# Sixteen small writes to the output ahead of the first load, on GpSimd's software queue

## The chip, the cores and the metric

The kernel runs on one core of a Trainium2 chip (trn2). Times are device microseconds (us) of that core; executions that agree within 1.5% of the fastest are fast. A packet below is one entry of the trace's record of the DMA engines, with its start, its length and its size. An "engine-us" is one microsecond of one of the sixteen DMA engines: 16 engine-us over all engines are 1 us of each.

## The reference, cut to what matters

```python
# attn_weights: (8, 12, 1024, 1024) float32;  v: (8, 12, 1024, 64) float32
def reference(attn_weights, v):
    return np.einsum('bhqs,bhsd->bhqd', attn_weights, v).astype(np.float32)
```

Almost all bytes are attention weights: 403 MB, read once. v and the output are 25 MB each.

## The kernel before

The 96 heads are handled four at a time, in 24 blocks. A block is a pair of attention loads (8.4 MB each in memory, cast to 16 bits on the way), one v load (1 MB) and one store (1 MB). GpSimd issues them all on its software queue, except the first v load and the last stores, which SyncE issues on its hardware queue. TensorE transposes the weights and multiplies.

```python
nc.vector.memset(ident, 0.0).then_inc(s_memset)
# ...
load_attn(0)                      # GpSimd, software queue
load_attn(1)
pool.wait_ge(s_memset, 2)
pool.affine_select(out=ident, ...)  # constants for TensorE
# ...
for n in range(NU - 2):
    pool.wait_ge(s_t[True], (n + 1) * PER_DVE)   # a buffer is free
    load_attn(n + 2)
    if n % 2 == 0:
        q = n // 2
        for s in s_sp:
            pool.wait_ge(s, 2 * q + 2)
        if q + 1 < NV:
            load_v(q + 1)
        if 0 < q <= HELD_FROM:
            store(q - 1)          # the first store: q = 1, at 79.5 us
# ...
nc.sync.dma_start(out=v32, in_=v_g[0]).then_inc(s_v0, 16)   # the first v, hardware queue
# ... at the end:
nc.sync.wait_ge(s_out, NU)
nc.sync.dma_start(out=outs[:, 0], in_=rows[:, 0]).then_inc(s_end, 16)
```

Of the kernel before, what the change touches and what calls it, by code (L numbers as in the profile page):

```python
# [10 lines left out]
def kernel(  # L11
# [18 lines left out]
    nc = tc.nc  # L30
# [16 lines left out]
    NV = NH // VH  # L47
# [12 lines left out]
    def slot(q):  # L60
        return q % 2 if q < 2 * BY_EIGHTS else q - 2 * BY_EIGHTS + 2

    attn_q = attn_weights.rearrange("b (hq four) (p r) s -> (b hq) (four p) (r s)", four=VH, p=VP)
    out_q = out.rearrange("b (hq four) (p r) d -> (b hq) (four p) (r d)", four=VH, p=VP)
    v_g = v.rearrange("b (hq four) (p r) d -> (b hq) (four p) (r d)", four=VH, p=VP)
# [11 lines left out]
    with tc.tile_critical(no_gpsimd_drain=True):  # L77
        sem = tc.alloc_semaphore
# [17 lines left out]
        s_second = {n: sem(f"s_second{n}") for n in range(HALVED, NU)}  # L96
        s_v0, s_v = sem("s_v0"), sem("s_v")
        s_osb = [sem(f"s_osb{i}") for i in range(NO)]
        s_end = sem("s_end")

        s_t = {True: sem("s_t_dve"), False: sem("s_t_act")}
        s_sp = [sem("s_sp_dve"), sem("s_sp_act")]
# [109 lines left out]
        def engine(dve):  # L212
# [11 lines left out]
            def back_copy(rows, j0, jn, ps, count):  # L224

                eng.wait_ge(s_back, count)
                return copy(  # L227
                    out=rows.rearrange("p (half j) d -> p j half d", half=2)[:, ds(j0, jn)],
                    in_=ps[:, ds(0, jn * P)].rearrange("p (j half d) -> p j half d", half=2, d=D),
                )  # L230

            def rows_of(n):
                return osb[slot(n // 2)][:, ds(n % 2 * G, G)]
# [51 lines left out]
            k = 1 - e  # L285
            back_copy(rows_of(NU - 1), 4 * k, 4, px[k], 2 * NU + k + 1).then_inc(s_fin[k])

        nc.vector.memset(ident, 0.0).then_inc(s_memset)
        nc.vector.memset(spread, 0.0).then_inc(s_memset)

# [23 lines left out]
        def store(q, by_sync=False):  # L314
# [12 lines left out]
            out=ident,  # L327
            in_=ident,
# [7 lines left out]
        for h in range(VH):  # L336
            pool.wait_ge(s_const, h + 1)
            pool.affine_select(  # L338
                out=spread[ds(h * VP, VP)],
                in_=spread[ds(h * VP, VP)],  # L340
# [39 lines left out]
            store(q, by_sync=True)  # L380
        rows = osb[slot(NV - 1)].rearrange("p (u half j) d -> p u half j d", u=2, half=2)
        outs = out_q[NV - 1].rearrange("p (u half j d) -> p u half j d", u=2, half=2, j=GH)
        nc.sync.wait_ge(s_out, NU)
        nc.sync.dma_start(out=outs[:, 0], in_=rows[:, 0]).then_inc(s_end, 16)
        for k in range(2):
# [36 lines left out]
```

## Time and profile before

| | before |
|---|---|
| time, median of the first 3 runs | 1055.67 us (1055.58 to 1055.79) |
| span of the profiled run | 1053.3 us |
| software queue's share of the sixteen engines | 99.4% |
| TensorE starts on the first load | 25.21 us |
| second pair of loads landed | 86.63 us |
| interval with the first store / with every later one | 45.06 / 43.56 us |

The lines behind these are in the prediction. TensorE's start tells when the first load landed. It is in the timeline (start, busy, engine, line, operation):

```profile
25.21 9.57 PE L124 MATMUL bank<-ident,abf 128*128 128x128 f32 x64 [25.21 <-DMA abf<-in_attn_weights_dram]
```

An interval is the time between the landings of two pairs of loads, each read from the chain in order of time as start plus length.

### The profile page before, as it was taken

To read this page: it belongs to the slowest core of one execution; us is meant where nothing else is said; L and a number is where in the kernel's file an instruction comes from. 1 tells how busy PE (TensorE), PEld (TensorE's weight loads), DVE (VectorE), ACT (ScalarE), POOL (GpSimd) and SP (SyncE) were. 2 spreads that over 40 slices of the span, in tenths; PEclk is the share of its full clock that TensorE was granted. 3 is DMA by queue.
4 is the path that set the end of the run, shared out by engine and by line. 5 is a ranking of instruction groups with operands and counts; after the bars stand their busy time and mean duration, and the time that the engine had idled before them with its cause. 6 is when DMAs were issued, how large, how long until landed. Compare 5 with 4: busy or idle time off the path is not lost.

```text
span 1053.3 us, 16277 instructions
## 1 busy us (share of the span) xinstructions
PE 754.8 (72%) x6920; PEld 709.4 (67%) x6920; DVE 387.9 (37%) x582; ACT 403.3 (38%) x489; POOL 52.4 (5%) x102
## 2 busy tenths in 40 slices
PE   0877686766867578775687766876678768777795
PEld 0776576766867568675686666866667668776785
DVE  1443343333443234432343333433335234433452
ACT  0443344433543334442353333433334334433452
POOL 1000000000000000000000000000000000000000
PEclk9989888888888888898888888888789898898898
DMA  9999999999999999999999999999999999999998
GB/s 219 220 217 208 234 236 218 238 209 247 233 218 238 207 243 239 217 238 209 244 236 215 234 219 237 238 219 234 227 228 234 215 218 218 218 218 215 210 217 322
DMA packets 14662, 239.67 MB, mean 228 GB/s; under 512 B 1600, under 2 KB 2112, under 8 KB 5184
## 3 DMA queue, kind: packets, MB, share of 16 engines
q0 software_dynamic: 13392, 234.36, 99.4%
q1 hardware_dynamic: 1264, 5.24, 1.3%
q8 instruction: 2, 0.03, 0.0%
q14 instruction: 4, 0.03, 0.0%
HBM read 427.82 MB, written 25.17 MB: 430 GB/s over the span
## 4 chain that ended last, share of the span: by engine, by line
DMA 76%; PE 23%; issue 1%; POOL 0%; DVE 0%; ACT 0%; SPq 0%; POOLq 0%
DMA abf<-in_attn_weights_dram 76%; PE bank L124 22%; PE bank L166 0%; PE bank L151 0%; POOL abf L304 0%; DVE osb L227 0%; ACT ot L256 0%; POOLq L417 0%; SPq L371 0%; SPq L77 0%
## 5 line engine op out<-in xcount | busy, mean ns | idle before, releaser
L124 PE MATMUL bank<-ident,abf 128*128 128x128 f32 x3072 | 470.8, 327 | 260.0 <-DMA abf<-in_attn_weights_dram 254.2
L124 PEld LDWEIGHTS bank<-ident,abf 128*128 128x128 f32 x3072 | 461.5, 215 | 272.8 <-DMA abf<-in_attn_weights_dram 266.7
L244 DVE COPY at<-bank 128x1024 bf16<-128x1024 bf16 x480 | 320.3, 689 | 495.1 <-PE bank L124 492.5
L244 ACT COPY at<-bank 128x1024 bf16<-128x1024 bf16 x288 | 289.2, 1012 | 428.1 <-PE bank L124 428.1
L166 PE MATMUL bank<-at,vbf 128*64 128x256 bf16 x3072 | 215.0, 278 | 0.0
L166 PEld LDWEIGHTS bank<-at,vbf 128*64 128x64 bf16 x3072 | 196.7, 108 | 13.4 <-DVE at L244 4.0
L256 ACT COPY ot<-bank 128x512 f32<-128x512 f32 x48 | 28.1, 586 | 181.1 <-PE bank L166 181.1
L256 DVE COPY ot<-bank 128x512 f32<-128x512 f32 x48 | 33.2, 692 | 151.4 <-PE bank L166 151.4
L151 PE MATMUL bank<-ident,ot 128*128 128x128 f32 x392 | 52.2, 276 | 33.0 <-DVE vbf L220 32.2
L151 PEld LDWEIGHTS bank<-ident,ot 128*128 128x128 f32 x392 | 43.4, 141 | 45.0 <-DVE vbf L220 44.0
L304 POOL DMA_DIRECT2D abf<-in_attn_weights_dram x50 | 26.6, 532 | 896.4 <-PE bank L124 895.3
L227 ACT COPY osb<-bank 128x512 f32<-128x512 f32 x97 | 52.2, 589 | 22.5 <-PE bank L151 22.5
L220 DVE CAST vbf<-bank 128x512 bf16<-128x512 f32 x48 | 30.9, 686 | 6.6 <-PE bank L139 6.6
L220 ACT CAST vbf<-bank 128x512 bf16<-128x512 f32 x48 | 25.8, 589 | 11.8 <-PE bank L139 11.8
L139 PE MATMUL bank<-vr,spread 32*128 32x512 bf16 x384 | 25.7, 377 | 0.0
L139 PEld LDWEIGHTS bank<-vr,spread 32*128 32x128 bf16 x384 | 9.9, 92 | 6.9
L310 POOL DMA_DIRECT2D vr<-in_v_dram x23 | 12.1, 528 | 19.2 <-PE bank L139 18.8
L317 POOL DMA_DIRECT2D out_dram<-osb x20 | 10.7, 537 | 37.3 <-ACT osb L227 37.3
L244 ACT ACT_TABLE_LOAD x8 | 10.3, 1283 | 1.2 <-SPq L77 1.1
L294 DVE CAST vr<-v 128x2048 bf16<-128x2048 f32 x1 | 1.4, 1406 | 3.3 <-DMA v<-in_v_dram 3.3
L338 POOL TENSOR_SCALAR_AFFINE_SELECT spread<-spread 32x512 bf16<-32x512 bf16 x4 | 2.5, 629 | 0.6
L227 DVE COPY osb<-bank 128x512 f32<-128x512 f32 x1 | 0.7, 692 | 3.1 <-PE bank L151 3.1
(8 smaller groups left out, 2.1 us busy)
## 6 DMA issues: line engine op xcount, KB each, us to landing
abf<-in_attn_weights_dram POOLq DMA_DIRECT2D x46, 4096.0 KB, 33.2
out_dram<-osb POOLq DMA_DIRECT2D x20, 1024.0 KB, 34.2
vr<-in_v_dram POOLq DMA_DIRECT2D x23, 512.0 KB, 34.3
abf<-in_attn_weights_dram POOLq DMA_DIRECT2D x4, 2048.0 KB, 26.0
out_dram<-osb SPq DMA_DIRECT2D x3, 1024.0 KB, 11.8
v<-in_v_dram SPq DMA_DIRECT2D x1, 1024.0 KB, 4.9
out_dram<-osb SPq DMA_DIRECT2D x1, 512.0 KB, 7.8
out_dram<-osb SPq DMA_DIRECT2D x2, 256.0 KB, 3.0
```

The source lines that it names most:

```text
L124: last = pe.matmul(out=pt[g % 4][:, k], lhsT=words[:, k], rhs=ident, is_transpose=True, start=(k == 0), stop=(k == KW - 1),)
L139: last = pe.matmul(out=ps, lhsT=spread[rows, b], rhs=vr[rows, b], start=(b == 0), stop=(b == VB - 1),)
L151: last = pe.matmul(out=ps[:, ds(j * P, P)], lhsT=ot[:, j0 + j], rhs=ident, is_transpose=True, start=(j == 0), stop=(j == jn - 1),)
L166: last = pe.matmul(out=outs, lhsT=vbf[:, 2 * kw + par, h], rhs=at[:, ds(half * GH, GH), kw, ds(h * VP, VP), par], start=(n == 0), stop=(n ...
L220: copy(out=vbf[:, :, h], in_=ps.rearrange("p (k d) -> p k d", k=SB)).then_inc(s_vbf[e])
L227: return copy(out=rows.rearrange("p (half j) d -> p j half d", half=2)[:, ds(j0, jn)], in_=ps[:, ds(0, jn * P)].rearrange("p (j half d) -> ...
L244: ins = copy(out=at[:, g].rearrange("c k j two -> c (k j two)"), in_=bank[g % 4].bitcast(bf16),)
L256: copy(out=ot.rearrange("c j (h p) -> c h j p", h=VH)[:, ds(2 * e, 2)], in_=po[e].rearrange("c (h j p) -> c h j p", h=2, j=GH),).then_inc( ...
L304: pool.dma_start(out=abf[n % 2][:, ds(g0, gn)].rearrange("p g s -> p (g s)"), in_=attn_q[n // 2][:, ds((n % 2 * G + g0) * S, gn * S)],).th ...
L310: pool.dma_start(out=vr.rearrange("p b x -> p (b x)"), in_=v_g[iv]).then_inc(s_v, 16)
L317: eng.dma_start(out=out_q[q], in_=osb[slot(q)].rearrange("p r d -> p (r d)"), **({} if by_sync else {"single_packet": True}),).then_inc(s_ ...
L338: pool.affine_select(out=spread[ds(h * VP, VP)], in_=spread[ds(h * VP, VP)], compare_op=mybir.AluOpType.not_equal, fill=1.0, base=0, patte ...
```

## The change

The sixteen pieces are 64 bytes each, one for each DMA engine, copied from v into places of `out` that the last stores overwrite. The intent: let every engine touch `out` once at the start, so that whatever a first write costs is paid early and not in the middle of the stream.

```diff
-        s_end = sem("s_end")
+        s_end, s_touch = sem("s_end"), sem("s_touch")
 # ... ahead of the first load on GpSimd:
+        nc.gpsimd.dma_start(
+            out=out_q[NV - 1].rearrange("(e p) x -> e p x", e=16)[:, 0, ds(0, 16)],
+            in_=v_g[0].rearrange("(e p) x -> e p x", e=16)[:, 0, ds(0, 16)],
+        ).then_inc(s_touch, 16)
 # ... before the last stores:
+        nc.sync.wait_ge(s_touch, 16)
         nc.sync.wait_ge(s_out, NU)
```

## The prediction

> **What bounds the kernel now.** I read the page first, for which resource is full.
>
> ```profile
> PE 754.8 (72%) x6920; PEld 709.4 (67%) x6920; DVE 387.9 (37%) x582; ACT 403.3 (38%) x489; POOL 52.4 (5%) x102
> q0 software_dynamic: 13392, 234.36, 99.4%
> HBM read 427.82 MB, written 25.17 MB: 430 GB/s over the span
> DMA 76%; PE 23%; issue 1%; POOL 0%; DVE 0%; ACT 0%; SPq 0%; POOLq 0%
> ```
>
> No compute engine is full, but packets of the software queue q0 take 99.4% of the span of the sixteen DMA engines, and the chain that ended last is 76% loads. The 23% of PE in that chain are transposes that free a buffer for the next load while another load already fills the engines. So time is bytes over rate: 427.82 + 25.17 = 453 MB at 430 GB/s give 1053 us. What matters is any stretch in which the engines do less than that.
>
> I then looked for such stretches. The chain in order of time (start, length, what) shows when pairs of loads land:
>
> ```profile
> 2.14 43.36 DMA abf<-in_attn_weights_dram
> ...
> 55.31 31.32 DMA abf<-in_attn_weights_dram
> ...
> 96.46 35.23 DMA abf<-in_attn_weights_dram
> ...
> 141.28 33.97 DMA abf<-in_attn_weights_dram
> ```
>
> Start plus length gives landings at 45.50, 86.63, 131.69 and 175.25, so intervals of 41.13, 45.06 and 43.56 us; the later ones with a store in them are also 43.56. The first interval has no store: 1 MB less, 2.4 us at 430 GB/s, accounts for 41.1. But the interval with the *first* store is 1.5 us longer than every later one. The stretches (bounds, length, each engine's busy time, PE clock, DMA share, GB/s delivered) compare its v load with the next pair's, each from its first packet:
>
> ```profile
> 104.20:105.20 1.00, 0.00 (x0) 0.00 (x0) 0.00 (x0) 0.00 (x0) 0.00 (x0) 0.50 0.88 139
> 105.20:106.20 1.00, 0.20 (x1) 0.20 (x2) 0.00 (x0) 0.00 (x0) 0.00 (x0) 0.50 1.12 123
> 106.20:107.20 1.00, 1.00 (x6) 1.00 (x6) 0.03 (x1) 0.00 (x0) 0.00 (x0) 0.50 0.78 115
> 148.60:149.60 1.00, 0.00 (x0) 0.00 (x0) 0.00 (x0) 0.00 (x0) 0.00 (x0) 0.50 0.56 111
> 149.60:150.60 1.00, 0.00 (x0) 0.00 (x0) 0.00 (x0) 0.00 (x0) 0.00 (x0) 0.50 0.93 188
> 150.60:151.60 1.00, 0.55 (x3) 0.55 (x4) 0.00 (x0) 0.00 (x0) 0.00 (x0) 0.50 1.08 266
> ```
>
> For 2.5 us the first delivers about half the rate of the second. The single packets say the same: a v packet takes 0.324 us everywhere, but here up to 0.96, an excess of 16 engine-us, or 1.0 us on each of 16 engines. No other stretch of the kernel has that much. The first store's packets follow at 107.5 us and themselves are normal (0.309 to 0.322 us).
>
> The timeline of the start (start, busy, queue) shows who issues first:
>
> ```profile
> 0.96 0.39 SPq L363 DMA_DIRECT2D v<-in_v_dram  x1
> 1.48 1.22 POOL L304 DMA_DIRECT2D abf<-in_attn_weights_dram  x2 [1.03 <-SPq L77]
> ```
>
> In the packet records the v load (queue q1) runs from 2.0 us; its first packets take 0.6 to 1.1 us, later ones 0.309. The first q0 packet starts at 5.04, on each engine 6 ns or so after that engine's last q1 packet (5.0 to 5.5). So **the first attention load waits for the v load, not for its own issue**.
>
> **What the Trainium skill says.** "DMA: Bandwidth & Descriptors", section "Where 436 GB/s comes from", puts the fabric ceiling at 435 GB/s; the trace's 430 agrees, and leaves an estimated 453 MB / 435 GB/s = 1041 us, so no change that leaves the bytes alone can gain much over 1%. The same page, "Specifications", says that software-issued transfers take about 1 us to the first byte and that pieces under 512 B are written by read-modify-write. The v load, hardware-issued, took 1.0 us from issue to first packet, longer than the 0.6 us given there; no run yet shows a small write. I found no page that names a cost for a first write to a tensor. "TensorE: Matmul & The Clock Gate", section "What's actually happening", says that the activity window is 3413 ns and runs free; the trace has a granted clock of 0.50 from 1034 us to about 1039.4 and 1.00 after.
>
> **The change part by part.** Nothing is removed. Added:
> 1. One issue on GpSimd ahead of the first load. An issue costs 0.49 to 0.73 us there (1.22 for two). The first load is issued near 2.0 instead of 1.48, its descriptors are ready at about 3.0 (estimate with the skill's 1 us), still before the v load ends at 5.04. On the path: **0 us**. The constants on GpSimd come 0.5 us later too, at 6.7 instead of 6.2; PE needs them at 25.2.
> 2. Sixteen packets of 64 B, one per engine by the 16-row pattern, with sixteen semaphore packets, ahead of the first load in the same queue. A 1 KB packet takes 0.046 us and a semaphore packet 0.022 in this trace, so **+0.07 us** if warm. If cold, like the first v packets (0.3 to 0.8 us over normal), **+0.3 to +0.8**.
> 3. A wait on SyncE near 1041 us, met since microsecond 6: 0. A branch on GpSimd: under 0.1 us, hidden as in 1.
> 4. If the 1.5 us at 104 is the engines' first write to out, the change pays that earlier: **-1.5**, less what it costs at the start. There the v load is running, so half-rate reads for 2.5 us could cost up to 1.2 again; or it overlaps the slow first v packets and costs little.
>
> A shift carries to the end one for one: the queue always holds another load (33 us to landing, against about 20 of transfer), and the tail follows the last landing at 1034.27.
>
> The sum: with the saving of 4, 1055.67 - 1.5 + 0.1 to 1.2, so 1054.3 to 1055.4. Without it, +0.1 to +0.8, so 1055.8 to 1056.5.
>
> **The rivals.** *First-write cost moved* (45%): for it speaks that the slow stretch comes just before the first store, whose descriptors had been waiting since 79.5 us, and never returns; against it, that it hits v reads and not the store's own packets. It gives about 1054.8. *Chance collision* (40%): around 104 us the engines, until then in step to within about 1 us, drift apart, and the v packets collide once with long reads. The touch then saves nothing except by chance: 1055.9. *The small write blocks the queue* (15%): read-modify-write and receipt hold each engine 1 to 2 us ahead of the first load, with no saving later: 1057. Against it, packets behind a store in this trace don't stall. On top lies the **clock phase in the tail**: the last transposes take 6.25 us because most run at clock 0.50; a shift against the free-running window could lengthen or shorten that by an estimated 1 us, though a gain stops at the DMA, which is 0.98 busy from 1034 to 1049.
>
> **Range and chances.** 0.45 x 1054.8 + 0.40 x 1055.9 + 0.15 x 1057 = 1055.6; I take 1055.4, as the first theory could pay more than I charge it. The range spans the full saving, 1054.1, to the blocking case, 1057.0. Two per cent is 21 us, more than the 12 us to the ceiling; a slowdown that large needs a lasting loss of rate from sixteen packets. Hence 0.98 for within 2%.
>
> **What would show it.** (1) The first load's landing (PE starts at 25.21 now) moves by 0.1 to 0.8 us, not by the issue's 0.5 plus more. (2) The landing interval with the first store drops from 45.06 to 43.56 if the first-write theory holds, and stays within 0.3 if not. (3) v at the start lands later than 4.9 us after issue if the cost moved there. (4) Later intervals stay at 43.56. (5) The tail from last landing to end keeps its 19 us. The prediction is wrong if the engines settle into another pattern with another steady interval: 0.5 us in each of 18 would be 9 us.

## More of the kernel before

"Slow engine-us" are the lengths of slow packets over their usual length, added up.

As the engines are always busy, intervals show where the run gains or loses. But a pair has landed only when the slowest of the sixteen engines is done. So an interval holds two things: what all engines lose, and how far the slowest falls behind the others.

## The result, and the profile after

| | before | after |
|---|---|---|
| time, median of 4 runs | 1055.73 us (1055.58 to 1056.07) | 1055.84 us (1055.79 to 1056.01) |
| ratio | | 1.0001, 95% interval 0.9984 to 1.0018 |
| span of the profiled run | 1053.3 us | 1053.6 us |
| TensorE starts on the first load | 25.21 us | 26.54 us |
| slow engine-us of loads in the first 10 us | 0.2 | 8.3 |
| interval with the first store | 45.06 us | 44.08 us |
| slow engine-us near the first store | 15.8 | 9.6 |

A ratio here is the mean time of one kernel's fast runs over that of the other's of the same rounds, so not quite the ratio of the medians in the table. The time is the same. But the two traces differ, in three places.

**The start.** The timeline after shows the added issue, the first load's issue 0.65 us later, and TensorE's start:

```profile
0.96 0.39 SPq L369 DMA_DIRECT2D v<-in_v_dram  x1
...
1.50 0.63 POOL L290 DMA_DIRECT2D out_dram<-in_v_dram  x1 [1.05 <-SPq L77]
...
2.13 1.10 POOL L310 DMA_DIRECT2D abf<-in_attn_weights_dram  x2
...
26.54 10.46 PE L124 MATMUL bank<-ident,abf 128*128 128x128 f32 x64 [26.54 <-DMA abf<-in_attn_weights_dram]
```

TensorE starts 1.33 us later. The stretches (bounds, length, busy time of PE, PEld, DVE, ACT, POOL, PE clock, DMA share, GB/s of packets that start there) show why. Each engine moves the first load in packets of usually 2.432 us; the second packets start here. Before:

```profile
7.40:8.10 0.70, 0.00 (x0) 0.00 (x0) 0.00 (x0) 0.00 (x0) 0.00 (x0) 1.00 3.48 749
8.10:9.40 1.30, 0.00 (x0) 0.00 (x0) 0.00 (x0) 0.00 (x0) 0.00 (x0) 1.00 0.00 0
```

After:

```profile
7.40:8.10 0.70, 0.00 (x0) 0.00 (x0) 0.00 (x0) 0.00 (x0) 0.22 (x1) 1.00 1.91 374
8.10:9.40 1.30, 0.00 (x0) 0.00 (x0) 0.00 (x0) 0.00 (x0) 0.00 (x0) 1.00 0.97 202
```

Before, all sixteen second packets start before 8.1 us: 749 GB/s for 0.7 us is sixteen packets of 32 KB. After, half of them do; the others come up to 9.3 us. The first packets took 2.43 to 3.55 us, and the last of them began at 6.36 instead of 5.54 us. The second packets are slow too: of the 8.3 slow engine-us, 5.6 lie in the first packets and 2.7 in the second. The small writes themselves took 0.011 us each with a semaphore packet of 0.009, between 5.02 and 5.55 us, each just behind its engine's last v packet. The v load is untouched (4.9 us to landing in both).

**The first store.** The chain in order of time after (start, length, what), answering to the lines that the prediction shows:

```profile
2.67 44.04 DMA abf<-in_attn_weights_dram
55.00 32.20 DMA abf<-in_attn_weights_dram
...
96.80 34.48 DMA abf<-in_attn_weights_dram
141.00 33.98 DMA abf<-in_attn_weights_dram
```

The landings are 46.71, 87.20, 131.28 and 174.98 us, so the interval with the first store is 44.08, 0.98 less than before. Its v load, from its first packet on, is slow still, for two of the three microseconds:

```profile
104.60:105.60 1.00, 0.00 (x0) 0.00 (x0) 0.00 (x0) 0.00 (x0) 0.00 (x0) 0.50 0.70 78
105.60:106.60 1.00, 0.00 (x0) 0.00 (x0) 0.00 (x0) 0.00 (x0) 0.00 (x0) 0.50 0.80 111
106.60:107.60 1.00, 0.93 (x5) 0.93 (x5) 0.00 (x0) 0.00 (x0) 0.00 (x0) 0.50 1.04 205
```

**Later intervals.** Before, all of them up to the last store on the software queue are 43.55 to 43.57. After, three are longer: 43.70, 43.77 and 43.98, together 0.77 us over.

**The account**, in landings after against before: the second pair +0.57 us (87.20 against 86.63); the interval with the first store -0.98; the later intervals +0.75; at the last landing +0.34 (1034.61 against 1034.27), and so in the span (+0.3). TensorE's +1.33 is the slowest engine alone, most of which is made up by the second pair.

The average over the engines tells more. Each engine ends a load with a semaphore packet, so the packet records hold all sixteen times. The average engine is 0.67 us later than before at the second landing (8.3 / 16 = 0.52 of it in slow packets), 0.14 at the third and 0.02 at the landing near 951 us. So at the first store it saved 0.53, not 0.98, which is less than it lost at the start. The longer later intervals cost it nothing: there the slowest engine falls further behind. First and last engine are 1.66 us apart at the third landing and 2.46 at the eighth (2.18 at both before).

### The profile page after: what moved, and what is told of

The parts are those of the page before. It is cut to its first block, busy times and chain, and to the rows that moved or that the text cites. A ratio compares the mean times of both kernels' runs of the same rounds, so it can differ in the third digit from the quotient of the medians.

```text
span 1053.6 us, 16279 instructions
## 1 busy us (share of the span) xinstructions
PE 753.3 (71%) x6920; PEld 708.0 (67%) x6920; DVE 387.5 (37%) x582; ACT 403.1 (38%) x489; POOL 53.8 (5%) x103
## 3 DMA queue, kind: packets, MB, share of 16 engines
q0 software_dynamic: 13424, 234.36, 99.3%
HBM read 427.82 MB, written 25.17 MB: 430 GB/s over the span
## 4 chain that ended last, share of the span: by engine, by line
DMA 76%; PE 23%; issue 1%; POOL 0%; DVE 0%; ACT 0%; POOLq 0%; SPq 0%
DMA abf<-in_attn_weights_dram 76%; PE bank L124 22%; PE bank L166 0%; PE bank L151 0%; POOL abf L310 0%; DVE osb L227 0%; POOL out_dram L290 0%; ACT ot L256 0%; POOLq L424 0%; SPq L377 0%; SPq L77 0%
```

## The experiments

Two questions: what makes the first load slow, and why does the first store cost less? The theory of the prediction, the first-write theory, answers both: an engine's first write to `out` costs something, once. Its rivals: the later issue of the first load; the small transfer as such; for the store, chance or the state of the engines. One execution of each kernel was profiled, and the times come from 2 to 5 runs of each changed kernel. The edits of e1 to e4 and e6 are against the changed kernel, that of e10 is shown against e3, and the others are against the kernel before. The kernels' results were all correct. Slow engine-us come from the packet records. Kernels are compared only within the same rounds.

| kernel | PE start, us | slow loads, first 10 us | interval with first store, us | slow near first store | time; before in the same call, us |
|---|---|---|---|---|---|
| before | 25.21 | 0.2 | 45.06 | 15.8 | 1055.73 |
| after | 26.54 | 8.3 | 44.08 | 9.6 | 1055.84; 1055.73 |
| e1 first-stored words | 26.10 | 8.9 | 44.15 | 6.6 | 1055.88; 1055.66 |
| e2 into SBUF | 26.09 | 8.3 | 44.07 | 6.1 | 1055.91; 1055.66 |
| e3 touch late | 25.20 | none | 45.04 | 16.8 | 1055.56; 1055.66 |
| e4 touch by ScalarE | 25.22 | none | 44.95 | 15.9 | 1055.72; 1055.66 |
| e5 short fill | 25.15 | none | 45.13 | 12.6 | 1055.62; 1055.56 |
| e6 touch behind two loads | 25.16 | none | 44.99 | 17.3 | 1055.80; 1055.56 |
| e7 blocks swapped | 25.04 | none | 45.02 | 16.3 | 1055.41; 1055.56 |
| e8 store ahead of v | 25.13 | none | 45.30 | 16.4 | 1055.60; 1055.56 |
| e9 longer fill | 25.21 | none | 45.18 | 15.5 | 1055.54; 1055.80 |
| e10 late touch from SBUF | 25.09 | 0.3 | 45.23 | 17.0 | 1055.92; 1055.80 |
| e11 first store by SyncE | 25.17 | none | see below | 6.4 and 7.9 | 1055.64; 1055.80 |
| e12 fill of 4 us | 27.21 | 10.5 | 45.24 | 12.3 | 1057.75; 1055.66 |

### Which words, which memory, which time, which queue

**e1**, the small writes to the words that are stored first:

```diff
-            out=out_q[NV - 1].rearrange(...)[:, 0, ds(0, 16)],
+            out=out_q[0].rearrange(...)[:, 0, ds(0, 16)],
 # in store():
+            if q == 0:
+                eng.wait_ge(s_touch, 16)
```

> The sixteen small writes go to words of out that are stored FIRST, not last; GpSimd waits for them before its first store. If each engine pays once for a place in out (so that touching the last block prepares only part of the first store), the first loads are slowed as in the changed kernel (PE starts near 26.5 us, not 25.2) and the interval with the first store falls from 44.08 to 43.6 us: time 1055.4. If any write does the same, or the slow stretch near 104 us is a chance collision, the interval stays between 44.0 and 45.1 and the time at 1055.8.

Measured: 8.9 slow engine-us at the start, an interval of 44.15, ratio 1.0003 (0.9987 to 1.0020). The interval did not fall further than with the last words (44.08). The place within `out` makes no difference that shows.

**e2**, the same packets into a scratch tile in SBUF:

```diff
+        scratch = sb("scratch", [16, 16], fp32)
-            out=out_q[NV - 1].rearrange(...)[:, 0, ds(0, 16)],
+            out=scratch,
```

> The same sixteen packets from v, but into a scratch tile in SBUF: the issue, the packets and the semaphores stay, the write to memory goes. First-write theory: PE starts at 25.2 to 25.3 us as in the kernel before, and the interval with the first store is back near 45.06; time 1055.7 to 1055.9. Issue-or-packets theory (the added issue or the small packets themselves delay the first load): PE starts near 26.5 us as in the changed kernel.

Measured: TensorE starts at 26.09, the interval is 44.07, ratio 1.0001. Nothing is written to `out` before the first store, and both effects are there all the same. This alone refutes the first-write theory, at the start and at the store. TensorE's start and the chain:

```profile
26.09 9.64 PE L125 MATMUL bank<-ident,abf 128*128 128x128 f32 x64 [26.09 <-DMA abf<-in_attn_weights_dram]
```

```profile
56.06 31.36 DMA abf<-in_attn_weights_dram
...
97.24 34.25 DMA abf<-in_attn_weights_dram
```

The stretches, as above:

```profile
7.40:8.10 0.70, 0.00 (x0) 0.00 (x0) 0.00 (x0) 0.00 (x0) 0.21 (x1) 1.00 0.45 94
8.10:9.40 1.30, 0.00 (x0) 0.00 (x0) 0.00 (x0) 0.00 (x0) 0.00 (x0) 1.00 1.68 353
```

Here nearly all second packets are late: 94 GB/s against 749 before, and 353 in the stretch in which there was none.

**e3**, the small writes behind the second block's v load instead of at the start:

```diff
-        nc.gpsimd.dma_start(out=out_q[NV - 1]..., in_=v_g[0]...)   # at the start
 # in the loop:
                 if q + 1 < NV:
                     load_v(q + 1)
+                if q == 0:
+                    pool.dma_start(out=out_q[NV - 1]..., in_=v_g[0]...).then_inc(s_touch, 16)
```

> The same small writes, issued behind the second pair's v load instead of first, so that they run near 67 us. First-write theory: PE starts at 25.2 and pair one lands at 45.5 as before, the slow packets come between 63 and 72 us, and the interval with the first store is near 44.1 as in the changed kernel; the second landing is up to 1.2 us late. Chance theory: nothing slow near 67 us, and the interval with the first store anywhere between 43.6 and 45.1.

Measured: they ran at 65.5 to 66.9 us, 0.024 us each, with no slow packet near them; TensorE starts at 25.20, and the interval is 45.04 with 16.8 slow engine-us. A first write to `out` by every engine, some 40 us ahead of the first store, neither costs nor saves.

**e4**, the same writes issued by ScalarE on its hardware queue:

```diff
-        nc.gpsimd.dma_start(
+        nc.scalar.dma_start(
```

> The same small writes issued on ScalarE's hardware queue at about 1.1 us, so that GpSimd's first load is issued at 1.48 again and the writes run at about 2 us, while the engines have only v to fetch. First-write theory with overlap: the first load is less slowed (PE starts at 25.2 to 25.8), v lands a little later than 4.9 us after issue, and the interval with the first store stays near 44.1: time 1054.7 to 1055.3. If the cost lies on each queue by itself: PE starts at 25.2 and the interval with the first store is 45.06 again, time 1055.7. If it can't be overlapped: PE starts near 26.5, time 1055.8.

Measured: they ran at 5.10 to 5.51 us, the very place that they have in the changed kernel, and not at 2 us as I had expected. TensorE starts at 25.22, the interval is 44.95. So a small write between v and the first load is not harmful as such; it is when it goes ahead of the load in the load's own, software queue.

### Later issue, or the transfer ahead

**e5**, no small writes, a fill by GpSimd ahead of the first load:

```diff
+        scratch = sb("scratch", [P, 512], fp32)
+        pool.memset(scratch, 0.0)
         load_attn(0)
```

> No small writes at all: the kernel before with a fill of a 128x512 scratch tile by GpSimd ahead of its first load, so that the load is issued some 0.5 to 1 us later. Late-issue theory (the first load was ready only just in time behind v, so any delay of its issue shows): its first packets are slow or late as in the changed kernel, PE starts at 26.0 to 26.6, and the slow v packets near 104 us shrink from 16 to 6 to 10 engine-us because the engines are then out of step. Software-packet theory (what slows the first load is a small software transfer just ahead of it): PE starts at 25.2 and the stretch near 104 us costs 16 engine-us, as before.

Inconclusive: the fill ran from 0.95 to 1.48, within a wait that GpSimd has anyway, and the load was issued at 1.51.

**e6**, the small writes behind the first two loads on the same queue:

```diff
         load_attn(0)
         load_attn(1)
+        nc.gpsimd.dma_start(out=out_q[NV - 1]..., in_=v_g[0]...).then_inc(s_touch, 16)
```

> The changed kernel with the small writes issued behind the first two loads and not ahead of them; they then run at about 45 us. Late-issue theory: first load issued at 1.48 again, PE starts at 25.2, pair one lands at 45.5, the interval with the first store is 45.0: everything as before, time 1055.7. First-write theory (already weakened): slow packets near 45 us and an interval near 44.1.

Measured: TensorE starts at 25.16, the interval is 44.99, nothing is slow between 43.6 and 45.1 us, where they ran; ratio 1.0002. So it takes being ahead of the first load. One later interval was 44.31.

**e9**, the fill again, with 1152 instead of 512 columns:

> The fill of the earlier delay run fitted into a wait that GpSimd had anyway (its first load was still issued at 1.51 us), so it tested nothing. Here it is 128x1152, long enough (an estimated 1.2 us from 0.95) that the first load is issued at 2.1 us as in the changed kernel, with no transfer added. Late-issue theory: the first packets are slow or late by some 8 engine-us, PE starts at 26.0 to 26.6, and the stretch near 104 us costs 6 to 10 engine-us. Software-packet theory (the small transfer itself slows what follows it): PE starts at 25.2, first packets normal, near 104 us 12 to 17 engine-us.

The timeline shows the fill and the load's issue at 1.95 us, 0.47 later than before and 0.18 earlier than in the changed kernel; the stretches show all second packets in time:

```profile
0.95 1.06 POOL L324 MEMSET scratch<- 128x1152 f32 x1 [0.51 <-SPq L77]
...
1.95 1.22 POOL L305 DMA_DIRECT2D abf<-in_attn_weights_dram  x2
```

```profile
7.40:8.10 0.70, 0.00 (x0) 0.00 (x0) 0.00 (x0) 0.00 (x0) 0.21 (x1) 1.00 3.47 749
8.10:9.40 1.30, 0.00 (x0) 0.00 (x0) 0.00 (x0) 0.00 (x0) 0.00 (x0) 1.00 0.00 0
```

TensorE starts at 25.21, with no slow load. A later issue alone is hidden behind v, as step 1 of the prediction has it. What remains is the small transfer ahead of the load in its queue. (e9's issue is still 0.18 us earlier than that of the changed kernel; e12 below closes this gap. The size of the transfer was not varied.)

**e12**, fills of two output buffers and a scratch tile, until v has left the engines:

```diff
+        for x in (osb[NO - 1], osb[NO - 2], scratch):
+            pool.memset(x, 0.0)
         load_attn(0)
```

> Again no small writes, only fills by GpSimd ahead of the first load, long enough (an estimated 4.3 us) that the load is issued near 5.2 us, after v has left the engines. It measures what lateness alone does. Its first packets should start at 5.2 us plus the way from issue to first packet: about 1 us by the earlier estimate, so PE starts near 26.1; if that way is 3 us, PE starts near 28.1. Carry step: the time grows by the same amount, 1056.5 or more. In-step theory: engines that start late but together keep full-length first packets (none stretched) and still pay 15 to 17 engine-us near 104 us. If lateness alone were what trades against the stretch near 104 us, that falls to 6 to 10 and the time stays near 1055.7.

The timeline:

```profile
4.91 1.21 POOL L305 DMA_DIRECT2D abf<-in_attn_weights_dram  x2
...
27.21 10.33 PE L125 MATMUL bank<-ident,abf 128*128 128x128 f32 x64 [27.21 <-DMA abf<-in_attn_weights_dram]
```

The load is issued at 4.91 and its first packets start at 6.29, so the way from issue to first packet is 1.38 us. I had expected full-length first packets, and that is wrong: they took 2.88 to 3.29 us on all sixteen engines, 10.5 slow engine-us, and the second packets are normal. So **the first load has a slow first packet of its own when it meets idle engines**. Issued at 1.48, it would by the same 1.38 us be ready near 2.9 us (an estimate), two microseconds before v leaves the engines, and there its first packets are of normal length. Even issued at 2.13, as in the changed kernel, it would be ready near 3.5 (an estimate), so lateness alone does not explain what happens there. A reading is that v covers this slow beginning in the kernel before, and that it is uncovered again in the changed kernel. The sums are of one size, 8.3 and 10.5 engine-us, but not the shapes: here all first packets are slow and no second one, while in the changed kernel four first packets carry 3.3 of the 8.3, and the second packets 2.7. That the small packets and their semaphores keep the engine from beginning the load early is the reading that fits e4, e6, e9 and e12; no run shows it directly.

The carry step holds: TensorE starts 2.0 us later than before, the last landing is 1.95 us later (1036.22), and the time is 1057.75 against 1055.66 (ratio 1.0020, 1.0006 to 1.0034). It is the only version whose time differs clearly from that of the kernel before.

### What the first store costs

**e7**, head blocks 2 and 5 in each other's place:

```diff
+        block = [{2: 5, 5: 2}.get(q, q) for q in range(NV)]
-                    in_=attn_q[n // 2][:, ...],
+                    in_=attn_q[block[n // 2]][:, ...],
 # v_g[iv] and out_q[q] likewise
```

> The kernel before with head blocks 2 and 5 handled in each other's place (loads, v and stores alike). If the slow v packets near 104 us belong to the place of v that is read there (block 2), they move to block 2's new time, near 235 us, or vanish, and the interval with the first store falls to 43.6. If they belong to that moment (the first store behind this v load, or the step of the engines), they stay near 104 us at about 16 engine-us and the interval is 45.06.

Measured: the slow packets stay near 104 us (16.3), the interval is 45.02. They don't belong to a place in v.

**e8**, the store ahead of the v load in each block:

```diff
+                if 0 < q <= HELD_FROM:
+                    store(q - 1)
                 for s in s_sp:
                     pool.wait_ge(s, 2 * q + 2)
                 if q + 1 < NV:
                     load_v(q + 1)
-                if 0 < q <= HELD_FROM:
-                    store(q - 1)
```

> The kernel before with each pair's store issued ahead of its v load. If a v load is slow because a first store follows it in the queue, the slow packets go over to other packets or vanish (interval 43.6 to 45.1, told by which packets are slow). If v loads collide when the engines are in step, the store ahead spreads or does not spread the engines: slow v packets remain near 107 us and the interval stays near 45. In the best case the interval is 43.6 with nothing slow elsewhere, and the time 1054.2.

Measured: no v packet is slow any more. Instead, some 16 attention packets ahead of the store are a microsecond too long each (16.4 in all); the interval is 45.30. So the cost goes with the place ahead of the first store, to v packets or to attention packets.

**e10**, the late touch with an SBUF source and the store's packet form:

```diff
-                        in_=v_g[0].rearrange(...)[:, 0, ds(0, 16)],
+                        in_=ident[ds(0, 16), ds(0, 16)],
+                        single_packet=True,
```

> The late touch again, near 65 us, but its sixteen pieces come from SBUF (a constant tile) and go to out, in the store's own packet form. If the engines pay once for the first transfer out of SBUF or in that form, the slow packets come near 63 to 66 us and the interval with the first store is 43.6. If what costs is the first large store, or the moment, nothing is slow near 65, and 104 us costs 16 engine-us with the interval at 45.0.

Measured: nothing slow near 65 us, 17.0 slow engine-us at the store, interval 45.23. A small transfer out of SBUF doesn't pay for the store either.

**e11**, the first store by SyncE as soon as it is ready (its semaphore bookkeeping is adapted, not shown):

```diff
-                if 0 < q <= HELD_FROM:
+                if 1 < q <= HELD_FROM:
                     store(q - 1)
 # SyncE, ahead of its waits for load 3:
+            if n == 1:
+                nc.sync.wait_ge(s_out, 3)
+                nc.sync.dma_start(out=out_q[0], in_=osb[0]...).then_inc(s_first, 16)
```

> The kernel before with its first store issued by SyncE's hardware queue at about 80 us, as soon as it is ready; the second store stays on GpSimd's queue and runs at about 151 us. If the cost belongs to the first store from whatever queue: slow packets at 79 to 84 us, none at 104 or 148. If it belongs to the software queue's first store: slow packets near 148 us. If it belongs to the moment: slow packets near 104 us still. In all three some 16 engine-us, one interval longer by about 1.5 us, and the time 1055.5 to 1055.8.

Measured: nothing is slow near 104 us. 6.4 slow engine-us of loads lie between 80 and 88 us, around the store on the hardware queue, and 7.9 between 140 and 160, around the software queue's first one. The two together are 14.3, about what one place had (of the 7.9, some 2 lie in loads behind the store). The landings are 45.56, 88.28, 131.21 and 175.07, so the sum of the three intervals is 129.51 us against 129.75 before, and the time is the same (ratio 0.9996, 0.9979 to 1.0012). So the cost does not belong to the moment near 104 us: it moved with the stores, and moving it gained nothing. That each queue's first store has a cost of its own fits this, but is not shown: most of the loads slow near 82 us ran beside the packets of SyncE's store (from 82.4), and no run shows what such sharing alone costs a load.

**What stays open.** The interval with the first store fell to 44.07 to 44.15 in exactly the three kernels with a small software transfer ahead of the first load, and was 44.95 to 45.30 in all others with an ordinary first store. For the average engine the gap is narrower: 43.99 to 44.21 in the three, 44.36 (e5) to 44.74 (before) in the others. Two readings are left. In the three the engines may be more out of step when they come to the first store: the last packets ahead of its v load end between 104.62 and 106.34 in the changed kernel, but for 14 engines between 104.18 and 104.69 in the kernel before, with two a microsecond later. From first to last engine that is 1.72 us against 1.52, though, and e6, which saved nothing, has 1.60 and e1 1.63, so this reading is weak. Or the software queue's own beginning is involved. e12 speaks against a third reading, that any late start trades against the store: it started later than all, and its interval is 45.24 (44.54 for the average engine). No run tells the first two apart.

Single later intervals are longer by 0.1 to 0.75 us: every kernel with small transfers has at least one, and before, e5, e7, e8, e9 and e12, without such transfers, have none; e11 has some too. In the changed kernel these are 43.57 to 43.59 for the average engine, so one or a few engines fall behind there. Why they do is not known.

No version beat the kernel before by more than the scatter.

## Why the prediction was right or wrong

The time, 1055.84, lies in the range and 0.4 us over the stated 1055.4; "within 2%" is right. This is no support for the mechanism: the kernel before, at 1055.73, lies in the same range, and the stated time weighs three theories, none of which came true as stated. The chain of steps is right only in parts.

- **The bound, and the carry.** Right. The software queue still has 99.3% of the engines, and e12's 2.0 us at the start are 1.95 at the last landing and 2.1 in the time. The tail stayed at 19.0 us from last landing to end of span (1053.6 - 1034.61), as stated. (The 430 GB/s that the prediction sets beside the ceiling count bytes at the memory. After the cast the packets write 228 GB/s on average. That the ceiling binds here rests on the two figures being close.)
- **Step 1, the later issue costs 0.** Right: e9's issue, 0.47 us later, left TensorE's start at 25.21.
- **Step 2, the sixteen packets.** The packets are even shorter than the small term: 0.020 us for write and semaphore in the trace, against 0.07. What failed is the place of the cold cost. I put +0.3 to +0.8 on the small packets; they are not slow at all, and the load behind them is, by 0.52 us in slow packets for the average engine and 1.33 us at TensorE's start. The first landing was thus to move by 0.1 to 0.8, and moved by more.
- **Step 3.** Right; no wait on it shows at the end.
- **Step 4, the saving of 1.5 us at the first store, charged with up to 1.2 at the start.** At the slowest engine 0.98 was saved, with +0.57 at the second landing; for the average engine 0.53 and +0.67, so the start took back all of the saving. The reading was loose, too: over their three microseconds the stretches at 104 and 148 us have a mean of 126 and 188 GB/s, so two thirds, and half only in the last two. The prediction's own sign, 43.56 or within 0.3 of 45.06, gave no answer: 44.08 is neither. The reason was wrong. e2 writes nothing to memory and has both effects; e3, e6 and e10 write to `out` well ahead of the first store and have neither. The charge was to come from a slower v load, and v lands 4.9 us after its issue as before. I had given this theory 45%.
- **The rival of a chance collision** falls too. The slow stretch came back in every run that has an ordinary first store, in e8 it went to other packets, and in e11 it moved with the store.
- **The rival of a blocked queue** comes nearest to the start: the small transfer does hold up the load behind it. But it holds up by 0.67 us per engine (at the second landing), not one or two, and not because of the write, which e2 doesn't have.
- **Later intervals at 43.56.** Three were not (+0.77 together at the slowest engine). The average engine lost nothing in them.

## What to carry to other kernels

Where the DMA engines are full from the first microseconds, look at what the *first* transfer of each queue hides behind: here the first software load runs at normal length behind a hardware-issued v load, but a kilobyte put ahead of it in its own queue, or an issue too late for v to cover it, cost it 8 to 11 engine-us. A one-time cost that shows once in the middle of a long stream is worth at most its own length (1.5 us of 1055 here), and moving it is not removing it. Where many engines share the work, take the average over them beside the slowest one: here half of a saving and all of a later loss were only the slowest engine's place. And test a reason by an experiment that keeps the mechanics and drops the supposed cause: the same packets into SBUF told more than any number of variations of the write.

## What the Trainium skill lacked or had wrong

- "DMA: Bandwidth & Descriptors" has no one-time cost of a queue's first transfers. Here the first v packets take 0.6 to 1.2 us (kernel before) instead of 0.309; the first attention packets, issued to idle engines, 2.88 to 3.29 us instead of 2.432; and packets ahead of the first store on that queue lose 12 to 17 engine-us once (15.8 in the kernel before; 6 to 10 in the three kernels with a small software transfer ahead of the first load).
- The same page, "Specifications", gives about 0.6 us to the first byte for hardware-issued and about 1 us for software-issued transfers. Here it was 1.0 us for the first v load (0.96 to 1.98) and 1.38 for a software load that met idle engines (4.91 to 6.29), counted from the start of the issuing instruction; counted from its end, 0.63 and 0.71. The page does not say from where it counts.
- The same section has pieces under 512 B written by read-modify-write. The 64-byte writes took 0.011 us in the packet record, as long as the equally small ones into SBUF in e2. No larger write was put in their place, so what the read-modify-write costs, if anything, no run here shows.
- No page tells that a small software transfer ahead of the first load in the same queue can slow that load's first packets: 8.3 to 8.9 engine-us in three kernels, none where it came behind the load or on another queue.
